# Row sums on one core: the last 8 rows of a partition in four loads of other sizes

## The chip, the cores and the metric

The kernel runs on 1 core of one Trainium2 chip. The metric is device time in microseconds (us) of one execution; the time before is the median of 3 runs. The profile is of one execution, and its times count from the first recorded instruction of that execution.

## The reference

```
def setup_inputs():
    batch, seq, dim = 32, 512, 1024
    return {"x": np.random.randn(batch, seq, dim).astype(np.float32)}

def reference(x):
    return np.sum(x, axis=-1).astype(np.float32)
```

The input has 32 x 512 = 16384 rows of 1024 float32 values (67.1 MB), and the output is one sum for each row (64 KB).

## The kernel before

The 16384 rows are spread over 128 partitions, 128 rows each. A row that is in SBUF is summed along its 1024 values by one of two engines, and the sums are collected in the tile `sums` (128 partitions x 128 values). Partition p holds 16 rows of a first region (the rows 0 to 15 of `sums`) and 112 rows of a second one (16 to 127); within a region the rows of a partition follow each other in DRAM, so that every load reads one contiguous run for each partition.

**Loads.** All loads of x are issued on SP's queue, in program order, into three rotating tiles `t` of 16 rows (and 4 values) each (pool `in`, `bufs=3`, line 145). The first load (lines 202 to 204) brings the first `FIRST` = 7 rows of the last 16; one of the hooks that run on the built program (lines 10 to 28) puts this load at the program's entry. Then come seven loads of 16 rows, g = 0 to 6 (lines 206 to 211, issued on line 192). The load of g = 1 is held until the first sum on DVE is done (line 213). What is left of the last 16 rows, 9 rows, comes as four loads: 6 rows (line 216), 2 rows (line 217), and the last row in two column pieces of 536 and 488 values (lines 227 and 228). A load into a tile waits until the tile's former user, three tiles back, has been read.

**Sums.** DVE sums the first 7 rows and the six groups g = 0 to 5 with one `tensor_reduce` each (`vec`, line 153). From g = 6 on, DVE takes single rows with `halves` (line 167): one instruction adds the two halves of a row and accumulates the total, so it runs over 512 elements for a row of 1024; a second small instruction reads the accumulator out. ACT takes whole rows with an activation that accumulates (`act`, line 180). Of g = 6, DVE has 9 rows and ACT 7; of the 6 rows, DVE 4 and ACT 2; of the 2 rows, one each. The last row is on DVE alone: the sum of its first 536 values is written as a `carry` into the cell in front of the 488 values, and the second `halves` sums that cell, the 488 values and one zeroed cell behind them (490 values, 245 elements; lines 223 to 233). The second instruction thus reads what the first one's accumulator read has written, and it waits for it by a semaphore of DVE's own.

**Stores.** ACT's queue issues two stores (lines 229 and 231): the 96 sums of the second region that are done by then, held until the load of 2 rows has landed, and the 16 sums of the first region. SP's queue issues the last store (line 234), the last 16 sums, when DVE and ACT have finished the rows. At the program's end GpSimd waits for that store to land (lines 55 to 98). The order on each engine is the order of the program text (`tc.manual_schedule()`).

Of the kernel before, what the change touches and what calls it, by code (L numbers as in the profile page):

```python
# [100 lines left out]
@with_exitstack  # L101
def kernel(
    ctx: ExitStack,
    tc: tile.TileContext,
    x: bass.AP,
    out: bass.AP,
):
    nc = tc.nc
    nc.at_finalize(issue_first_load_at_entry)
    nc.at_finalize(order_waits)  # L110
    nc.at_finalize(wait_for_the_store_at_the_clear)
    fp32 = mybir.dt.float32
    P = 128
    batch, seq, dim = x.shape
    rows = batch * seq
    J = rows // P
    BIG = 16


    x_r = x.flatten_outer_dims()  # L120
    out_r = out.rearrange("b s -> (b s)")
    ONE = BIG
    TWO = J - ONE

    def region(first, n):
        lo, hi = first * P, (first + n) * P
        return (
            x_r[lo:hi, :].rearrange("(p j) d -> p j d", j=n),
            out_r[lo:hi].rearrange("(p j) -> p j", j=n),
        )  # L130

    x_a, out_a = region(0, ONE)
    x_b, out_b = region(ONE, TWO)

    def rows_from(j, n):
        if j < ONE:
            return x_a[:, j : j + n, :]
        return x_b[:, j - ONE : j - ONE + n, :]

    last = J // BIG - 1  # L140
    FIRST = 7
    pieces = (536, 488)

    with (
        tc.tile_pool(name="in", bufs=3) as inpool,
        tc.tile_pool(name="unread", bufs=4, space=bass.MemoryType.PSUM) as upool,
        tc.tile_pool(name="stage", bufs=1) as stpool,
        tc.manual_schedule(),
    ):
        sums = stpool.tile([P, J], fp32)  # L150

        def vec(dst, src):
            return nc.vector.tensor_reduce(  # L153
                out=dst, in_=src, axis=mybir.AxisListType.X, op=mybir.AluOpType.add
            )

        def hold(inst, until, reason):
            tc.add_manual_dep(
                inst.ins,
                until.ins.name,  # L160
                mybir.DependencyInfo(mybir.DependencyClass.Sync, mybir.DependencyReason.DATA),
                reason=reason,
            )

        def halves(dst, src):
            n = src.shape[-1] // 2
            return nc.vector.tensor_tensor_reduce(  # L167
                out=src[:, :n],
                in0=src[:, :n],
                in1=src[:, n:],  # L170
                scale=1.0,
                scalar=0.0,
                op0=mybir.AluOpType.add,
                op1=mybir.AluOpType.add,
                accum_out=dst,
            )

        def act(dst, src, n):
            unread = upool.tile([P, dim], fp32)
            nc.scalar.activation(  # L180
                out=unread[:, :n],
                in_=src,
                func=mybir.ActivationFunctionType.Copy,
                accum_out=dst,
            )

        sums_of = []

        def rows(t, a, n, j, n_act, pairs=False):
            nv = n - n_act  # L190
            block = t[:, a * dim : (a + n) * dim].rearrange("p (n d) -> p n d", d=dim)
            load = nc.sync.dma_start(out=block, in_=rows_from(j, n))  # L192
            if pairs:
                for q in range(nv):
                    sums_of.append(halves(sums[:, j + q : j + q + 1], block[:, q, :]))
            else:
                sums_of.append(vec(sums[:, j : j + nv], block[:, :nv, :]))
            for q in range(nv, n):
                act(sums[:, j + q : j + q + 1], block[:, q, :], dim)
            return load  # L200

        j = last * BIG
        t = inpool.tile([P, BIG * dim + 4], fp32)
        rows(t, 0, FIRST, j, 0)
        first = sums_of[-1]
        for g in range(last):
            t = inpool.tile([P, BIG * dim + 4], fp32)
            if g < last - 1:
                load = rows(t, 0, BIG, g * BIG, 0)
            else:  # L210
                rows(t, 0, BIG, g * BIG, 7, pairs=True)
            if g == 1:
                hold(load, first, "no descriptors of later loads while the first ones start")

        t = inpool.tile([P, BIG * dim + 4], fp32)
        rows(t, FIRST, 6, j + FIRST, 2, pairs=True)
        two = rows(t, FIRST + 6, 2, j + FIRST + 6, 1, pairs=True)
        a = BIG - 1

        j += a
        c, width = pieces
        whole = t[:, a * dim + c : BIG * dim + 2]
        nc.vector.memset(whole[:, width + 1 :], 0.0)  # L225
        part = t[:, a * dim : a * dim + c]
        nc.sync.dma_start(out=part, in_=rows_from(j, 1)[:, 0, :c])  # L227
        nc.sync.dma_start(out=whole[:, 1 : width + 1], in_=rows_from(j, 1)[:, 0, c:])
        early = nc.scalar.dma_start(out=out_b[:, : TWO - BIG], in_=sums[:, ONE : J - BIG])
        hold(early, two, "its packets come behind those of the loads")  # L230
        nc.scalar.dma_start(out=out_a, in_=sums[:, :ONE])
        halves(whole[:, :1], part)
        halves(sums[:, j : j + 1], whole)
        nc.sync.dma_start(out=out_b[:, TWO - BIG :], in_=sums[:, J - BIG :])


# [28 lines left out]
```

## Time and profile before

| what | value |
|---|---|
| time, median of 3 runs (lowest to highest) | 161.54 us (161.33 to 161.68) |
| span of the profiled execution | 159.5 us |
| what lies between that span and the median | 2.0 us |
| DVE busy | 120.6 us (76%) in 40 instructions |
| ACT busy | 11.9 us (7%) in 21 instructions |
| SP's load queue, share of the 16 DMA engines | 97.8%, 67.12 MB |

The span runs from the first to the last instruction of the profiled execution; no time of that execution other than its span is listed, so the 2.0 us outside it is taken from the median. The chain of work that ended last is followed back from the last instruction, at each step to what released it. A `halves` shows as two records, `CUSTOM_DVE_ANT_0` (the sum) and `DVE_READ_ACCUMULATOR2_ANT` (the read-out, some 0.08 us). A load "lands" when the last of its completion counts has arrived.

### The profile page before, as it was taken

What the parts mean: (1) busy time and instruction counts of PE and PEld (TensorE: products, weight loads), DVE (VectorE), ACT (ScalarE), POOL (GpSimd) and SP (SyncE); (2) the same over time, 40 slices, a digit from 0 to 9 for tenths busy, and PEclk for the clock granted to TensorE, in tenths of its full rate; (3) what the DMA queues carried; (4) which work ended last, traced back from release to release, by engine and by line L of the source; (5) the groups of instructions that cost most, each with busy time, mean ns of one, the idle gap of its engine ahead of it and who ended that gap; (6) DMA issues with size and microseconds to landing.
All of it is one profiled execution on the core that took longest, in us unless ns stands there. A gap on an engine that the chain in (4) does not pass through costs nothing.

```text
span 159.5 us, 133 instructions
## 1 busy us (share of the span) xinstructions
DVE 120.6 (76%) x40; ACT 11.9 (7%) x21; POOL 0.2 (0%) x4
## 2 busy tenths in 40 slices
DVE  0029600499985999779995899949999499994955
ACT  3000000000000000000000000000000000003993
POOL 0000000000000000000000000000000000000000
DMA  8899989799699699699699699897996996996993
GB/s 316 388 479 526 411 378 526 329 460 526 279 509 526 263 526 526 263 526 526 263 526 493 296 526 427 362 526 345 444 526 279 509 526 263 526 526 283 407 384 125
DMA packets 2160, 67.18 MB, mean 421 GB/s; under 512 B 624, under 2 KB 752, under 8 KB 880
## 3 DMA queue, kind: packets, MB, share of 16 engines
q1 hardware_dynamic: 1872, 67.12, 97.8%
q10 hardware_dynamic: 288, 0.06, 0.2%
HBM read 67.11 MB, written 0.07 MB: 421 GB/s over the span
## 4 chain that ended last, share of the span: by engine, by line
DMA 71%; DVE 27%; SPq 1%; issue 0%; DVEq 0%
DMA t<-in_x_dram 71%; DVE sums L153 26%; SPq L192 0%; SPq L227 0%; DVE t L167 0%; DVEq L260 0%
## 5 line engine op out<-in xcount | busy, mean ns | idle before, releaser
L153 DVE TENSOR_REDUCE sums<-t 128x16 f32<-128x16384 f32 (+1 forms) x7 | 110.9, 15849 | 33.2 <-DMA t<-in_x_dram 33.2
L180 ACT ACTIVATE unread<-t 128x1024 f32<-128x1024 f32 x10 | 10.1, 1011 | 144.6 <-DMA t<-in_x_dram 144.6
L167 DVE CUSTOM_DVE_ANT_0 t<-t 128x512 f32<-128x512 f32 (+2 forms) x16 | 9.6, 657 | 4.0 <-DMA t<-in_x_dram 3.8
L180 ACT ACTIVATION_READ_ACCUMULATOR unread<-t 128x1 f32 x10 | 1.9, 186 | 0.0
L180 ACT ACT_TABLE_LOAD x1 | 1.3, 1283 | 0.8 <-PEq L249 0.8
L167 DVE DVE_READ_ACCUMULATOR2_ANT sums<- 128x1 f32 x15 | 1.3, 84 | 0.0
L249 POOL MEMSET const-bfloat16-1.0<- 128x1 bf16 x1 | 0.1, 101 | 0.0
L249 POOL MEMSET const-uint8-127<- 128x1 uint8 x1 | 0.1, 101 | 0.0
L249 POOL MEMSET const-float32-0.0<- 128x1 f32 x1 | 0.1, 98 | 0.2 <-issue 0.2
L249 POOL MEMSET const-float32-1.0<- 128x1 f32 x1 | 0.1, 98 | 0.0
L167 DVE DVE_READ_ACCUMULATOR2_ANT t<- 128x1 f32 x1 | 0.1, 81 | 0.0
L225 DVE MEMSET t<- 128x1 f32 x1 | 0.1, 59 | 0.0
## 6 DMA issues: line engine op xcount, KB each, us to landing
t<-in_x_dram SPq DMA_DIRECT2D x1, 3584.0 KB, 10.8
t<-in_x_dram SPq DMA_DIRECT2D x1, 3072.0 KB, 28.7
t<-in_x_dram SPq DMA_DIRECT2D x1, 1024.0 KB, 30.9
t<-in_x_dram SPq DMA_DIRECT2D x1, 268.0 KB, 31.0
t<-in_x_dram SPq DMA_DIRECT2D x1, 244.0 KB, 31.2
t<-in_x_dram SPq DMA_DIRECT2D x7, 40.8
out_dram<-sums ACTq DMA_DIRECT2D x1, 48.0 KB, 1.6
out_dram<-sums ACTq DMA_DIRECT2D x1, 8.0 KB, 1.5
```

The costliest lines, as they stand in the source:

```text
L153: return nc.vector.tensor_reduce(out=dst, in_=src, axis=mybir.AxisListType.X, op=mybir.AluOpType.add)
L167: return nc.vector.tensor_tensor_reduce(out=src[:, :n], in0=src[:, :n], in1=src[:, n:], scale=1.0, scalar=0.0, op0=mybir.AluOpType.add, op ...
L180: nc.scalar.activation(out=unread[:, :n], in_=src, func=mybir.ActivationFunctionType.Copy, accum_out=dst,)
L225: nc.vector.memset(whole[:, width + 1 :], 0.0)
L249: nc = _bacc.Bacc("TRN2", target_bir_lowering=False, num_devices=1)
```

## The change

`FIRST` becomes 8, so that 8 rows of 1024 values = 8192 values are left for each partition. They are taken as one run of values, with no regard to rows, in four loads of 5504, 1920, 512 and 256 values. Row boundaries are at 1024, 2048 and so on, so that row 5 (5120 to 6143) is cut at 5504, and row 7 (7168 to 8191) at 7424 and at 7936. Rows 3, 4 and 6 of the eight go to ACT, and the other five to DVE. Between two loads the tile has a gap of 2 cells: one zeroed, and one for the carry of the part of the row in front of it. A `halves` over the later part of a cut row starts at these two cells. Of g = 6, ACT has 6 rows in place of 7, and DVE 10 in place of 9.

The built program has on DVE, behind the 10 rows of g = 6: three memsets of one cell, `halves` of 512, 512, 512 and 192 elements (rows 0, 1, 2 and the first part of 5), then 321 and 128 (the rest of 5, the first part of 7), 257 (the second part of 7) and 129 (its last part). The 321, the 257 and the 129 each wait both for a load and for the carry of the `halves` that wrote it. On SP the four loads stand where four loads stood; on ACT 9 activations stand in place of 10, with the two stores behind them. In the text the two stores are now issued between the third and the fourth load, and the first is held until the load of 1920 values has landed.

```
-    FIRST = 7
-    pieces = (536, 488)
+    FIRST = 8
+    GAP = 2
+    LATE = ((0, 5504, (3, 4)), (5504, 1920, (6,)), (7424, 512, ()), (7936, 256, ()))
+    assert sum(n for _, n, _ in LATE) == (BIG - FIRST) * dim
...
+        def loads_end(q):
+            return LATE[q][0] + LATE[q][1]
...
-                rows(t, 0, BIG, g * BIG, 7, pairs=True)
+                rows(t, 0, BIG, g * BIG, 6, pairs=True)
...
+        j += FIRST
+        flat = rows_from(j, BIG - FIRST).rearrange("p n d -> p (n d)")
         t = inpool.tile([P, BIG * dim + 4], fp32)
-        rows(t, FIRST, 6, j + FIRST, 2, pairs=True)
-        two = rows(t, FIRST + 6, 2, j + FIRST + 6, 1, pairs=True)
-        a = BIG - 1
-        j += a
-        c, width = pieces
-        whole = t[:, a * dim + c : BIG * dim + 2]
-        nc.vector.memset(whole[:, width + 1 :], 0.0)
-        part = t[:, a * dim : a * dim + c]
-        nc.sync.dma_start(out=part, in_=rows_from(j, 1)[:, 0, :c])
-        nc.sync.dma_start(out=whole[:, 1 : width + 1], in_=rows_from(j, 1)[:, 0, c:])
-        early = nc.scalar.dma_start(out=out_b[:, : TWO - BIG], in_=sums[:, ONE : J - BIG])
-        hold(early, two, "its packets come behind those of the loads")
-        nc.scalar.dma_start(out=out_a, in_=sums[:, :ONE])
-        halves(whole[:, :1], part)
-        halves(sums[:, j : j + 1], whole)
+        for q, (at, _, _) in enumerate(LATE[1:], 1):
+            nc.vector.memset(t[:, at + (q - 1) * GAP : at + (q - 1) * GAP + 1], 0.0)
+        loads = []
+        for q, (at, n, on_act) in enumerate(LATE):
+            shift = q * GAP
+            loads.append(nc.sync.dma_start(out=t[:, at + shift : at + shift + n], in_=flat[:, at : at + n]))
+            if q == 2:
+                early = nc.scalar.dma_start(out=out_b[:, : TWO - BIG], in_=sums[:, ONE : J - BIG])
+                hold(early, loads[1], "its packets come behind those of the loads")
+                nc.scalar.dma_start(out=out_a, in_=sums[:, :ONE])
+            while at < loads_end(q):
+                row = at // dim
+                stop = min((row + 1) * dim, loads_end(q))
+                total = sums[:, j + row : j + row + 1]
+                if row in on_act:
+                    act(total, t[:, at + shift : stop + shift], dim)
+                else:
+                    start = at + shift - (GAP if at % dim else 0)
+                    whole = stop % dim == 0
+                    carry = t[:, stop + shift + 1 : stop + shift + 2]
+                    halves(total if whole else carry, t[:, start : stop + shift])
+                at = stop
         nc.sync.dma_start(out=out_b[:, TWO - BIG :], in_=sums[:, J - BIG :])
```

## Prediction

> **What bounds the kernel now.** I read the chain of work that ended last first. From the span's start it goes load, sum, load, sum, and from 126.16 us on it is this (columns: start, length, what):
>
> ```profile
> 125.68 0.43 SPq L227
> 126.11 0.04 issue
> 126.16 31.16 DMA t<-in_x_dram
> 157.32 0.02 issue
> 157.34 0.42 DVE t L167
> 157.76 0.01 DVEq L260
> ```
>
> The last load lands at 157.32, one sum of 0.42 us follows, and the last store goes out. The sums that the chain names earlier (DVE, 26% of the span) are not the limit. The table by stages shows it; the first row is one group of 16 rows, from landing to landing, and the others are the stages between the landings of g = 6, of the 6 rows, of the 2 rows, of the 536 and of the 488 values (columns: window, length, busy time with instruction count of DVE, ACT and POOL, clock, DMA share, GB/s):
>
> ```profile
> 107.55:126.91 19.36, 17.22 (x1) 0.00 (x0) 0.00 (x0) 1.00 1.00 433
> ...
> 146.26:153.56 7.30, 5.60 (x18) 7.28 (x14) 0.00 (x0) 1.00 0.99 425
> 153.56:156.07 2.51, 2.48 (x8) 2.21 (x5) 0.00 (x0) 1.00 0.98 398
> 156.07:156.73 0.66, 0.66 (x4) 0.64 (x1) 0.00 (x0) 1.00 0.86 330
> 156.73:157.32 0.59, 0.47 (x5) 0.51 (x2) 0.00 (x0) 1.00 0.33 89
> ```
>
> The DMA engines are full until the last packets (share 1.00 in the middle), and DVE needs 17.22 of 19.36 us. So the bytes set when the last data lands, and the change moves the same bytes. What it can alter is the packets' overhead and the **tail**: what is left to do when the last data has landed. The tail is in the timeline (start, length, engine, line, operation):
>
> ```profile
> 156.09 0.69 DVE L167 CUSTOM_DVE_ANT_0 t<-t 128x512 f32<-128x512 f32 x1
> 156.71 0.08 DVE L167 DVE_READ_ACCUMULATOR2_ANT sums<- 128x1 f32 x1
> 156.74 0.06 DVE L225 MEMSET t<- 128x1 f32 x1
> 156.75 0.44 DVE L167 CUSTOM_DVE_ANT_0 t<-t 128x268 f32<-128x268 f32 x1
> 157.05 0.19 ACT L180 ACTIVATION_READ_ACCUMULATOR unread<-t 128x1 f32 x1
> 157.11 0.08 DVE L167 DVE_READ_ACCUMULATOR2_ANT t<- 128x1 f32 x1
> 157.34 0.42 DVE L167 CUSTOM_DVE_ANT_0 t<-t 128x245 f32<-128x245 f32 x1
> 157.68 0.08 DVE L167 DVE_READ_ACCUMULATOR2_ANT sums<- 128x1 f32 x1
> 157.79 0.35 SPq L234 DMA_DIRECT2D out_dram<-sums  x1
> ```
>
> Two things are to be seen. An independent sum starts when the read-out of the sum before it starts (from 156.09 to 156.71 is 0.61, though the record is 0.69 long). But the 245-element sum depends on the carry of the 268: the read-out ended at 157.195, and the sum started at 157.344, 23 ns after the landing at 157.321. Between them stands DVE's wait for its own semaphore, which the records put at 157.234 with 21 ns. So a **hand-over** g from the end of one `halves` to the start of the next that reads its carry is at least 0.06 us (157.255 less 157.195) and at most 0.15. In this kernel the data comes last anyway, and the hand-over costs nothing.
>
> **Part 1, bytes and packets.** Each load has one packet for each partition, 8 on each of 16 engines, one behind the other. Landing to landing, divided by 8, gives the price of one: 24576 B (6 rows) 7.30/8 = 0.912; 8192 B 2.51/8 = 0.313; 2144 B 0.66/8 = 0.082; 1952 B 0.59/8 = 0.074. Between these, 22016 B (5504 values) is 0.819, 7680 B 0.295 and 2048 B 0.078. 1024 B lies between the 384 B packets of the early store (0.022) and 1952 B: 0.043 on the line, 0.022 to 0.074 as bounds. Times 8: 6.55, 2.36, 0.62 and 0.34, in sum 9.87. Before, the four took 157.32 - 146.26 = 11.06. The first load has packets of 32768 B in place of 28672 B: at 27.3 B per ns (from the 8192 and 24576 B prices) +0.150 each, +1.20 in all. Sum: 9.87 + 1.20 - 11.06 = 0.01, that is zero: **the last data lands at 157.32 as before** (157.2 to 157.6 by the bounds on 1024 B). The landings from which the rest is worked out: g = 6 at 146.26 + 1.20 = 147.46; 5504 at 154.01; 1920 at 156.37; 512 at 156.99; 256 at 157.32.
>
> **Part 2, the front.** The first load lands at 10.79 + 1.20 = 12.0, its sum of 8 rows takes 7.62 + 1.07 = 8.7 and ends at 20.7 in place of 18.43. The held load of g = 1 is issued 2.3 us later; g = 0 is in flight until 31.4, so this is hidden by 10 us. All groups shift by 1.20, DVE's idle of 2.1 us before each stays, and SP issues the four late loads at about 126.0 to 127.8 (0.43 each), 20 us ahead of their first packet. Cost: nothing.
>
> **Part 3, the last group and the 5504 values.** DVE: 10 rows from 147.48, 0.613 apart, end at 153.7 and the three memsets at 153.9; ACT: 6 rows of 1.04 end at 153.7. Both are ready before 154.01. Cost nothing; the cover is 0.1 to 0.3 us, and if it were gone, what is late would first use up the slack below. From 154.04 DVE runs three rows (1.84) and the 192 elements (record 0.36) to 156.24; with the hand-over it is ready for the 321 at 156.30 to 156.39, against a landing at 156.37. ACT's rows 3 and 4 end at 156.15.
>
> **Part 4, the tail.** A sum from its start to that of its read-out is 0.613 (512), 0.364 (268) and 0.339 (245 elements): 1.03 ns for an element and 0.088 fixed, near the 0.06 to 0.085 of the rows with one element (memset, read-out). So 321: 0.417; 257: 0.352; 128: 0.219; 129: 0.220; the read-out adds 0.081. For the two smallest no row exists; the bounds are 0.08 (one element) and 0.339 (245), and I take the line, as it meets the rows at both ends. DVE from the landing of the 1920 values:
> - 321 starts at 156.39; the independent 128 follows at 156.81 and ends, with its read-out, at 157.11
> - 257 needs that carry: it starts at 157.11 + g and takes 0.433. Its data landed at 156.99, so the carry decides
> - 129 needs the carry of the 257: it starts at 157.54 + 2g and takes 0.301. Its data landed at 157.32; again the carry decides
> - end 157.84 + 2g, against 157.76 before: **+0.08 + 2g**
>
> The bounds on g give +0.20 to +0.38. I take g = 0.09: a waiting instruction started 23 ns after its semaphore, and ACT's store record started 38 ns behind its wait record, so 0.06 + 0.03. That makes **+0.26**. What is queued behind the waiting sums on DVE is only the rest of this chain, and SP's last store waits for it. The bounds on 128 and 129 add -0.28 to +0.24, though below -0.08 the landing and ACT set the end.
>
> Beside it: ACT's row 6 starts at 156.39, takes 1.03 and its read-out to 157.54, hidden under DVE's 158.02. The two stores on ACT's queue go out 0.30 later (156.48, 156.89) and land at about 158.08 and 158.42; their packets start 0.9 after issue, at 157.36, behind the last load's packets, and the last store lands at about 159.48, so they are hidden. From SP's issue to the end it is as before, 159.53 - 157.79 = 1.74.
>
> Sum: span 159.53 + 0.26 = 159.79. The median shown lies 2.01 above the span, and I take that as fixed: **161.80 us**, +0.16%. The three runs shown spread over 0.35 us; 0.2% of the time (0.32 us) is about what a measurement of this kernel can tell from no change.
>
> **A rule to weigh.** The trace has dependent sums once, with g between 0.06 and 0.15, and independent ones that overlap by 0.08. The Trainium skill, VectorE: DVE Perf Modes, section "The DRAIN you can't avoid", says that each DVE instruction waits for the pipe to empty in any case, so that a semaphore between two of them costs nothing extra. By it, g would be what independent sums show. That is the first rival; the wait record that ends 0.06 after the read-out speaks against it.
>
> **Rivals.**
> - *The hand-over is free.* With g = 0 the end is +0.08 (161.62); with the overlap of independent sums, the 257 starts at 157.03, the 129 at 157.38, and the end is 157.68, -0.08 (161.46). Then the shorter last sum is a gain of a tenth of a us. For it: DVE is a queue in order. Against: the wait record. Chance 0.15.
> - *The hand-over or the small sums are dear: slower.* Place: between the 128 and the 257 and between the 257 and the 129. Price: at g = 0.15 the end is +0.38 (161.92). With the two small sums at the price of 245 elements and g = 0.09 it is +0.50 (162.04). It decides from g = 0.12, where +0.08 + 2g passes 0.32. For it: the trace allows 0.15, and a wait that finds its semaphore set is not seen there. Chance 0.27.
> - *The stream lands late.* If 1024 B cost as much as 1952 B, the last data lands 0.25 later, at 157.57, and the 129 would start at 157.72 anyway: hidden. Only if the 1920 values are late (packets to cells shifted by 8 B, or a slow first load) does it move the tail, one for one: 0.2 late is 162.0. Against: the 488 values, put one cell off, cost no more per byte than the 536. Chance 0.05.
>
> **How the numbers follow.** The forecast, +0.20 to +0.32, has 0.53; the rivals have 0.15, 0.27 and 0.05. Faster by over 0.2% needs 161.2: no mechanism above reaches it, only the spread of the runs on top of the free hand-over, 0.07. Slower by over 0.2%: the two dear cases, with the forecast's upper edge and the spread, 0.38. Within: 0.55. The range takes in both ends, with the spread at the low one: 161.35 to 162.10.
>
> **What would show it.** Right: landings near 147.46, 154.01, 156.37 and 157.32; a 257-element sum that starts about 0.09 after the 128's read-out has ended, not 0.02 after its landing; the same before the 129; DVE's last record ending near 158.02 and the chain naming DVE, not DMA, for the last 1.6 us. Wrong: a 129 that starts right behind the last landing, a span below 159.5, or a last landing over 0.4 us later.

## The result and the profile after

The changed kernel takes **162.18 us** (median of 4 runs, 162.15 to 162.21), against 161.52 for the kernel before (4 runs, 161.33 to 161.68). The ratio is 1.0042, with a 95% interval of 1.0031 to 1.0054: slower by 0.66 us, 0.4%. The forecast was 161.80 in a range of 161.35 to 162.10, most likely within 0.2%. The direction of the working was right, and the size was not: the time lies above the range.

The chain of work that ended last, in the profile after (start, length, what), from the issue of the load of 1920 values on:

```profile
126.47 29.98 DMA t<-in_x_dram
156.46 0.02 issue
156.48 0.49 DVE t L171
156.97 0.01 DVE sums L171
156.98 0.22 DVE t L171 x2
157.20 0.03 issue
157.23 0.02 DVEq L171
157.25 0.08 issue
157.34 0.45 DVE t L171 x2
157.78 0.03 issue
157.81 0.02 DVEq L171
157.83 0.08 issue
157.91 0.29 DVE t L171
158.21 0.01 DVEq L276
```

Before, the chain came to its last sum from the last landing. Now it leaves the DMA at the landing of the 1920 values, 156.46, and stays on DVE: four sums, and twice the same stretch of 0.03 issue, 0.02 wait on DVE's sequencer (DVEq) and 0.08 issue. That is the hand-over. Neither of the two landings that come later is in the chain. The stages between the landings of g = 6 and of the four loads (window, length, DVE, ACT, POOL, clock, DMA share, GB/s), behind one full group:

```profile
108.82:128.18 19.36, 17.22 (x1) 0.00 (x0) 0.00 (x0) 1.00 1.00 433
147.56:154.10 6.54, 6.24 (x23) 6.35 (x12) 0.00 (x0) 1.00 1.00 426
154.10:156.46 2.36, 2.20 (x8) 2.19 (x4) 0.00 (x0) 1.00 0.97 397
156.46:157.15 0.69, 0.67 (x4) 0.67 (x1) 0.00 (x0) 1.00 0.50 171
157.15:157.45 0.30, 0.16 (x3) 0.30 (x2) 0.00 (x0) 1.00 0.00 1
```

The lengths of 6.54, 2.36, 0.69 and 0.30 are near those worked out (6.55, 2.36, 0.62 and 0.34), and the last data lands at 157.45. The tail in the timeline after (DVE and SP):

```profile
156.90 0.29 DVE L171 CUSTOM_DVE_ANT_0 t<-t 128x128 f32<-128x128 f32 x1
...
157.11 0.08 DVE L171 DVE_READ_ACCUMULATOR2_ANT t<- 128x1 f32 x1
157.34 0.43 DVE L171 CUSTOM_DVE_ANT_0 t<-t 128x257 f32<-128x257 f32 x1
...
157.69 0.08 DVE L171 DVE_READ_ACCUMULATOR2_ANT t<- 128x1 f32 x1
157.91 0.29 DVE L171 CUSTOM_DVE_ANT_0 t<-t 128x129 f32<-128x129 f32 x1
158.13 0.08 DVE L171 DVE_READ_ACCUMULATOR2_ANT sums<- 128x1 f32 x1
158.24 0.35 SPq L250 DMA_DIRECT2D out_dram<-sums  x1
```

By the records of the packed trace, which go to the ns, the 128's read-out ends at 157.191 and the 257 starts at 157.335; the 257's ends at 157.770 and the 129 starts at 157.914. Both hand-overs are **0.144 us**.

SP's last issue moved from 157.795 to 158.243, 0.45 later, and the span from 159.5 to 160.0. The time grew by 0.66. The rest lies **outside the span**: each run comes with its time and its span (to 0.1 us), and in the four runs after, time less span is 2.15 to 2.21 us. For the kernel before it is 1.73 to 1.83 in all the runs of the experiments. So the two profiles explain 0.4 to 0.5 us, and the remainder needs another cause.

### The profile page after: what moved, and what is told of

Read it like the earlier page. It is cut to its first block, busy times and chain, and to the rows that moved or that the text cites. A ratio compares the mean times of both kernels' runs of the same rounds, so it can differ in the third digit from the quotient of the medians.

```text
span 160.0 us, 138 instructions
## 1 busy us (share of the span) xinstructions
DVE 121.9 (76%) x46; ACT 11.0 (7%) x19; POOL 0.2 (0%) x4
## 4 chain that ended last, share of the span: by engine, by line
DMA 71%; DVE 28%; issue 0%; SPq 0%; DVEq 0%
DMA t<-in_x_dram 71%; DVE sums L157 27%; DVE t L171 1%; SPq L232 0%; DVEq L171 0%; DVEq L276 0%; DVE sums L171 0%
## 5 line engine op out<-in xcount | busy, mean ns | idle before, releaser
L184 ACT ACTIVATE unread<-t 128x1024 f32<-128x1024 f32 x9 | 9.1, 1014 | 145.9 <-DMA t<-in_x_dram 145.9
L171 DVE CUSTOM_DVE_ANT_0 t<-t 128x512 f32<-128x512 f32 (+5 forms) x18 | 9.8, 598 | 2.9 <-DMA t<-in_x_dram 2.6
```

Source lines behind the costliest of these rows:

```text
L171: return nc.vector.tensor_tensor_reduce(out=src[:, :n], in0=src[:, :n], in1=src[:, n:], scale=1.0, scalar=0.0, op0=mybir.AluOpType.add, op ...
L184: nc.scalar.activation(out=unread[:, :n], in_=src, func=mybir.ActivationFunctionType.Copy, accum_out=dst,)
```

## The experiments

The first theory was that the hand-overs cost the 0.4 us of the tail, and that the rest was the place of one profiled execution within the spread of the kernel before. The rival was the front: that the larger first load delays the stream, or the program's start.

**The kernel before, unchanged.**

> The kernel before, unchanged, to see how its profile and time differ from one execution to the next. Both theories: 161.5 us. The hand-over theory explains 0.37 of the 0.66 us that the change cost (two waits of 0.144 us and 0.08 of work between the landing of the 1920 values and the last store); the rest, 0.13 us of later landings and 0.2 us outside the span, would be the place of one profiled execution of the kernel before within its spread of 0.35 us. Then this profile's span is 159.3 to 159.6 and time less span is about 2.2, as it was for the changed kernel. The front theory (the larger first load delays the stream and the start) has time less span at 2.0 here.

Measured: 161.41 us (11 runs) against 161.44 (32 runs), ratio 0.9992 to 1.0010; time less span 1.75 to 1.83. That part of my expectation failed: the kernel before has 1.8 us outside the span in every run, so the 2.2 us of the changed kernel are no spread of one execution. The chain's end in this profile:

```profile
157.38 0.06 issue
157.44 0.42 DVE t L167
157.85 0.01 DVEq L260
```

The last sum started 0.06 after the last landing, not 0.02. By the records, the 268's read-out ended at 157.293, and 0.145 later is 157.438, where the sum started. In this execution the hand-over decided in the kernel before as well, by 0.04.

**One part at a time: the front alone, the tail alone.** The first puts the old tail behind a first load of 8 rows:

```
-    FIRST = 7
+    FIRST = 8
-                rows(t, 0, BIG, g * BIG, 7, pairs=True)
+                rows(t, 0, BIG, g * BIG, 6, pairs=True)
-        rows(t, FIRST, 6, j + FIRST, 2, pairs=True)
-        two = rows(t, FIRST + 6, 2, j + FIRST + 6, 1, pairs=True)
+        rows(t, FIRST, 5, j + FIRST, 2, pairs=True)
+        two = rows(t, FIRST + 5, 2, j + FIRST + 5, 1, pairs=True)
```

> The first load of 8 rows and 6 rows of the last group on ACT, as changed, but the tail of before: 5 rows, 2 rows, 536 and 488 values. Hand-over theory: the 245-element sum again starts at the last landing, so 161.5 us, within 0.1 of before. Front theory (the larger first load is what costs): 161.8 to 162.2 us.

Measured: 161.43 us, ratio 0.9996 to 1.0013. The front costs nothing that shows. The second starts from the changed kernel:

```
-    FIRST = 8
+    FIRST = 7
-    LATE = ((0, 5504, (3, 4)), (5504, 1920, (6,)), ...
+    LATE = ((0, 1024, ()), (1024, 5504, (4, 5)), (6528, 1920, (7,)), (8448, 512, ()), (8960, 256, ()))
-                rows(t, 0, BIG, g * BIG, 6, pairs=True)
+                rows(t, 0, BIG, g * BIG, 7, pairs=True)
-            if q == 2:
+            if q == 3:
-                hold(early, loads[1], ...
+                hold(early, loads[2], ...
```

> The first load of 7 rows as before and 7 rows of the last group on ACT, then one row in a load of its own, and the four late loads of 5504, 1920, 512 and 256 values as changed. Hand-over theory: the tail costs 0.37 us, 161.9 us, with the 257 and the 129 elements starting 0.144 us after the read-outs before them. Front theory: 161.5 us.

Measured: 161.83 us, 0.39 over the kernel before, ratio 1.0015 to 1.0035; time less span 1.8. The tail alone costs what the hand-over theory says (0.37 us and 161.9 were expected), and the front theory falls.

**One hand-over more in the kernel before.**

```
-    pieces = (536, 488)
+    pieces = (280, 256, 488)
...
+        halves(second[:, :1], part)
-        halves(whole[:, :1], part)
+        halves(whole[:, :1], second)
         halves(sums[:, j : j + 1], whole)
```

> The kernel before with the last row in three pieces of 280, 256 and 488 values, each sum reading the carry of the one before, in place of 536 and 488. Nothing else is changed, and the last piece is the same. Hand-over theory: 140 elements end at 157.04, 129 start at 157.19, 245 at 157.63, end 158.05, that is 0.29 us over before, 161.8 us. If hand-overs were free, the 245 would start at the last landing as before: 161.5 us.

Measured: 161.71 us, 0.27 over before, ratio 1.0008 to 1.0025. The chain shows the two stretches of 0.13, with nothing of the changed kernel's loads in it:

```profile
157.25 0.03 issue
157.28 0.02 DVEq L167
157.30 0.08 issue
157.38 0.31 DVE t L167 x2
157.69 0.03 issue
157.72 0.02 DVEq L167
157.74 0.08 issue
157.83 0.41 DVE t L167
```

**The changed kernel again, beside its own parts.** The next four ran on one chip.

> The changed kernel, unchanged, beside runs of the kernel before on the same chip. The first result had 2.2 us outside the span in each of four runs, where the runs of the last four kernels had 1.8. If that is a matter of the chip or session and not of the program, 1.8 us lie outside the span here too, and the change costs what its tail costs: 0.37 us by the hand-over theory, 161.8 us against 161.44. If it belongs to the program, 162.1 us or more.

Measured: 162.16 us against 161.33, ratio 1.0035 to 1.0059; time less span 2.16 to 2.24. The 2.2 us belong to the program. Beside 23 runs of the kernel before, the change costs 0.83 us, about one half in the span and one half outside it. The 0.66 of the result rests on four runs of the kernel before that spread over 0.35 us. The next kernel swaps the order of two waits, in the hook that sorts them (`order_waits`):

```
+            if isinstance(inst, mybir.InstCustomDveAnt) and any(
+                (w.ant_name or "").startswith(("DMAHW2", "DMAHW3")) for w in inst.sync_info.on_wait
+            ):
+                insts[k] = with_first(inst, "DVE")
-            if isinstance(inst, (mybir.InstActivation, mybir.InstCustomDveAnt)):
+            elif isinstance(inst, (mybir.InstActivation, mybir.InstCustomDveAnt)):
```

> The changed kernel with the two waits of the 257 and of the 129 elements in the other order: the load's wait goes ahead as an instruction of its own, and the wait for the carry rides on the sum itself. Both waits are kept. If the 0.144 us of a hand-over is mostly the way from a wait instruction that ends late to the sum behind it, a sum that carries the wait itself starts some 0.035 us after the read-out (0.012 to the semaphore, 0.023 to the start), each hand-over is 0.11 shorter, and the time is 161.6 us. If it is the dependence itself, the pipe that has to empty, nothing changes: 161.8 us.

Measured: 161.96 us, 0.20 under the changed kernel beside it (6 and 5 runs, whose ranges overlap). The forecast time of 161.6 was missed, since 2.2 us lie outside the span here as well and not 1.8; what the two hand-overs lost is in its timeline:

```profile
157.14 0.08 DVE L175 DVE_READ_ACCUMULATOR2_ANT t<- 128x1 f32 x1
157.31 0.43 DVE L175 CUSTOM_DVE_ANT_0 t<-t 128x257 f32<-128x257 f32 x1
...
157.66 0.08 DVE L175 DVE_READ_ACCUMULATOR2_ANT t<- 128x1 f32 x1
157.78 0.29 DVE L175 CUSTOM_DVE_ANT_0 t<-t 128x129 f32<-128x129 f32 x1
```

The second hand-over is 157.781 less 157.746, 0.035 us, for the same dependence. The first is 0.09, because the load's own wait now stands ahead: it ended at 157.227, 0.05 after the landing at 157.177, and the sum started 0.084 after it. So most of the 0.144 is the wait as an instruction of its own, with the 0.084 from its end to the next start; the dependence alone leaves 0.035. The two hand-overs lost 0.16 us together, where 0.22 was expected.

The next kernel has one hand-over less:

```
-                    start = at + shift - (GAP if at % dim else 0)
+                    start = at + shift - (GAP if at % dim and q != 2 else 0)
-                    carry = t[:, stop + shift + 1 : stop + shift + 2]
+                    cell = LATE[3][0] + 2 * GAP if stop == LATE[2][0] else stop + shift + 1
+                    carry = t[:, cell : cell + 1]
```

> The changed kernel in which the 512 values are summed without the carry of row 7's first part (256 elements, no wait on DVE); that carry goes to the cell that was the zero in front of the last 256 values, so the last sum reads two carries. One hand-over of two is left behind the 1920 values' landing. Hand-over theory: the 256 elements start at their landing, 157.17, in place of 157.34, and the end is 0.17 us earlier: 161.6 us. If hand-overs were not the price, 161.8 us.

Measured: 161.59 us. That is the time expected, but in part by luck: of the 0.57 us under the changed kernel, 0.4 come from outside the span (1.8 here), which the working did not have, and the span's median is 0.2 shorter (159.8 for 160.0). In its profile, of an execution whose stream came later, the 256 elements start 0.024 after their landing and the last sum 0.144 after the read-out ahead of it, as the theory has it. The last one reads no carry at all (`start = at + shift`):

> The changed kernel with the carries written but not read: the sums of rows 5 and 7 of the last eight leave out their earlier parts. The loads, the pieces and the number of sums are the same, and no sum waits for another. Hand-over theory: the last sum starts at or just behind the last landing and is shorter than before's, so 161.36 us, 0.08 under before and 0.45 under the changed kernel. If the loads' sizes or the number of sums are the price, 161.7 to 161.8 us.

Measured: 161.32 us against 161.33, ratio 0.9991 to 1.0008; time less span 1.8. The same loads and pieces with no hand-over run as fast as the kernel before, though their sums leave out parts of two rows. Its timeline:

```profile
157.19 0.43 DVE L171 CUSTOM_DVE_ANT_0 t<-t 128x256 f32<-128x256 f32 x1
157.47 0.19 ACT L184 ACTIVATION_READ_ACCUMULATOR unread<-t 128x1 f32 x1
157.54 0.08 DVE L171 DVE_READ_ACCUMULATOR2_ANT t<- 128x1 f32 x1
157.54 0.29 DVE L171 CUSTOM_DVE_ANT_0 t<-t 128x128 f32<-128x128 f32 x1
```

The last sum starts together with the read-out ahead of it, 0.08 after the last landing (157.46): here DVE's own pace sets the end.

**The 0.4 us outside the span.** So far two programs had 2.2 us outside the span, the changed kernel and the one with swapped waits. Both have 58 instructions on DVE, counted in the built program with waits, branches and closing instructions (the traces record two fewer in every program); the others have 51, 55 and 59. The next four add memsets of cells that nobody reads, in DVE's idle time behind the first sum, so that nothing else moves:

```
         first = sums_of[-1]
+        pad = stpool.tile([P, 8], fp32)
+        for q in range(1):
+            nc.vector.memset(pad[:, 2 * q : 2 * q + 1], 0.0)
```

> The changed kernel with one more instruction on DVE: a memset of one cell that nobody reads, behind the first sum, where DVE idles for 11 us. So far the time less the span is 2.2 us for the two programs with 58 instructions in DVE's program (the changed kernel with its waits in either order) and 1.8 us for those with 51, 55 and 59. Theory of the place: the number of DVE's instructions decides what lies outside the span, with 3 left over after division by 4 at 1.8 and 2 left over at 2.2. This one has 59: 1.8 us outside, 161.75 us in all, 0.4 under the changed kernel, at the same span of 160.0. Rival: the 0.4 us belongs to the two hand-overs behind each other at the end of DVE's program: 2.2 us, 162.15 us.

> The kernel before with three such memsets, 54 instructions on DVE, 2 left over after division by 4. Theory of the place: 2.2 us outside the span, 161.8 us. Rival (the hand-overs, or the changed tail): 1.8 us, 161.4 us.

> The kernel before with one such memset, 52 instructions on DVE, none left over after division by 4. Theory of the place: another value than 1.8 us is possible, between 1.4 and 2.6, and if it is below 1.8 this beats the kernel before. Rival: 1.8 us, 161.4 us.

> The kernel before with two such memsets, 53 instructions on DVE, 1 left over after division by 4. Theory of the place: between 1.4 and 2.6 us outside the span. Rival: 1.8 us, 161.4 us.

Measured: the changed kernel with one memset more takes **161.72 us** (ratio to the kernel before 1.0009 to 1.0042), 0.4 less than without it on another chip, with 1.8 us outside (59 instructions). The rival, two hand-overs behind each other at the program's end, falls, since they are still there. But 52, 53 and 54 instructions in the kernel before all have 1.8 (161.34, 161.44 and 161.33 us, no ratio's interval clear of 1), so the remainder after division by 4 was wrong too. Three kernels more (the memset of the second on GpSimd, `nc.gpsimd.memset`):

> The kernel before with seven memsets of cells that nobody reads, behind the first sum: 58 instructions on DVE, as the changed kernel has. If the exact number of DVE's instructions puts 0.4 us outside the span, 2.2 us lie there and the time is 161.8 us at an unchanged span of 159.6. If it takes the changed tail as well, 1.8 us, 161.4 us.

> The changed kernel with such a memset on GpSimd in place of DVE: DVE keeps 58 instructions, the whole program has two more (GpSimd's memset and a wait of SP's at the end). If DVE's number decides, 2.2 us outside the span, 162.15 us. If the whole program's number or place decides, 1.8 us, 161.75 us.

> The changed kernel with two such memsets on DVE: 60 instructions there. If 58 alone is an unlucky number, 1.8 us outside the span, 161.75 us. If even numbers of the changed kernel are, 2.2 us, 162.15 us.

Measured: the kernel before with 58 instructions takes 161.77 us, ratio 1.0006 to 1.0030, at a span of 159.6 and with 2.16 to 2.22 outside. Its chain ends as that of before, so that the span tells nothing of the 0.4 us:

```profile
157.38 0.02 issue
157.41 0.42 DVE t L167
157.82 0.01 DVEq L263
```

With the extra memset on GpSimd the changed kernel keeps 2.2 (162.10 us), and with 60 instructions on DVE it has 1.88 to 1.96 (161.86 us). All three programs have 140 recorded instructions in all, so the whole program's number does not decide; DVE's does, in either kernel. The last three:

> The kernel before with six memsets on DVE, 57 instructions there. If what lies outside the span hangs on single numbers (58 at 2.2, 59 at 1.8, 60 at 1.9), 57 can be anything from 1.8 to 2.2 us; 1.8, as at 55 and below, would make 58 the first such number: 161.4 us. 161.8 us if 57 has it as well.

Measured: 161.77 us, ratio 1.0016 to 1.0036, 2.13 to 2.22 outside: 57 instructions have the 0.4 us too.

> The changed kernel with the two waits of the last two sums in the other order, and one memset more on DVE (59 instructions). In the profile of swapped_waits the 257 started 0.09 and the 129 0.035 us after the read-outs before them, in place of 0.144 each. Hand-over theory: 0.16 us less than after_plus1, 161.55 us. If the end does not hang on the hand-overs: 161.7 us.

Measured: 161.56 us, 1.8 outside: 0.16 under after_plus1, as expected, though that one ran on another chip (0.18 and 0.33 over the kernel before beside each). The ratio to the kernel before is 1.0007 to 1.0025.

> The changed kernel with one hand-over (as in one_handover, 55 instructions on DVE), and the last sum's two waits in the other order, so that this hand-over is 0.035 us in place of 0.144. Hand-over theory: 0.11 us less than one_handover, 161.48 us, within 0.1 of the kernel before. If the order of the waits did nothing: 161.6 us.

The edit is that of swapped_waits for the last sum alone. Measured: 161.43 us against 161.38, ratio 0.9992 to 1.0009. Its chain's end:

```profile
157.38 0.02 issue
157.40 0.09 DVE t L175
157.49 0.02 issue
157.51 0.29 DVE t L175
157.81 0.01 DVEq L281
```

One hand-over is left, with 0.02 of issue in place of 0.13. The changed loads then cost nothing, but no version here is faster than the kernel before.

**Where the 0.4 us lies.** The chains end with the last instruction, but the packed traces also hold the updates of semaphores behind it. In every profile the last of them are nine updates of semaphore 2, which no instruction of the kernel names; they begin 1.55 us after the last instruction's end. Between the fifth and the sixth lie 0.10 us with up to 55 and with 59 instructions on DVE, and 0.52 in all five profiles with 58. With 60, the third and the fourth lie 0.19 apart instead of 0.04. The updates of this semaphore in the last 0.4 us ahead of the span agree to 0.003 in all of them. So with 58 and 60 the extra time is spent at the program's end, behind the last instruction. The profile with 57 shows neither gap, though its execution had 2.2 us outside the span: there the place stays open.

All runs at a glance (medians; outside: time less span):

| kernel | DVE instructions | time | before beside it | span | outside |
|---|---|---|---|---|---|
| before, again | 51 | 161.41 | 161.44 | 159.6 | 1.8 |
| first load of 8, old tail | 51 | 161.43 | 161.44 | 159.6 | 1.8 |
| before + 1, + 2, + 3 memsets | 52, 53, 54 | 161.34, 161.44, 161.33 | 161.39 | 159.5 to 159.7 | 1.8 |
| before + 6 memsets | 57 | 161.77 | 161.38 | 159.6 | 2.2 |
| before + 7 memsets | 58 | 161.77 | 161.37 | 159.6 | 2.2 |
| before, three pieces | 55 | 161.71 | 161.44 | 159.9 | 1.8 |
| changed, the result | 58 | 162.18 | 161.52 | 160.0 | 2.2 |
| changed, again | 58 | 162.16 | 161.33 | 160.0 | 2.2 |
| changed + 1 on GpSimd | 58 | 162.10 | 161.37 | 159.9 | 2.2 |
| changed + 1, + 2 memsets | 59, 60 | 161.72, 161.86 | 161.39, 161.37 | 159.9 | 1.8, 1.9 |
| first load of 7, new tail | 59 | 161.83 | 161.44 | 160.0 | 1.8 |
| swapped waits | 58 | 161.96 | 161.33 | 159.8 | 2.2 |
| swapped waits + 1 memset | 59 | 161.56 | 161.38 | 159.8 | 1.8 |
| one hand-over | 55 | 161.59 | 161.33 | 159.8 | 1.8 |
| one hand-over, swapped | 55 | 161.43 | 161.38 | 159.6 | 1.8 |
| no carry | 55 | 161.32 | 161.33 | 159.5 | 1.8 |

## Why the prediction was right and wrong, point by point

- **The bytes and packets: right.** "The last data lands at 157.32 as before": it landed at 157.45, and every stage was within 0.07 of its length. The 0.1 us came with the front, and the kernel before varies by half as much (157.32 and 157.38 in its two profiles).
- **The front and the last group cost nothing: right** (first8_old_tail, 161.43 against 161.44).
- **The tail, +0.08 + 2g: right in form.** DVE's sums took 0.49, 0.29, 0.43 and 0.29, as worked out, the end hung on the two carries, and the chain named DVE. With g = 0.144 the formula gives +0.37; first7_new_tail, which has the tail alone, measured +0.39, and after_plus1 +0.33.
- **g = 0.09: this step failed in size.** It was "0.06 + 0.03", with the 0.03 from two other rows (0.023 from a semaphore to a sum, 0.038 from a wait to a store on ACT). What lies between DVE's wait record and the next DVE start is 0.084, so g is 0.144, at the upper bound that the trace of before gave (0.15). That bound had hardly any slack: 157.255 + 0.084 = 157.339 is within 0.005 of where the last sum started before (157.344), so there the hand-over and the landing came almost together. I took the hand-over to be hidden behind the landing, and the row showed nearly its whole length.
- **"The median shown lies 2.01 above the span, and I take that as fixed": this step failed.** The 2.01 were one profiled execution against the median of others. The kernel before has 1.8, which the fastest of the three runs shown also gives (161.33 less 159.5). And it is not fixed: it is 2.2 in every kernel run with 57 or 58 instructions on DVE, and the change took DVE from 51 to 58. That is 0.4 us, about as much as the tail costs.
- **How the two add up.** The forecast was 159.79 + 2.01, and the profiled execution after has 160.0 + 2.2. Of the 0.38 us between them, half is in the span: 0.11 from g, and 0.09 because the 1920 values landed at 156.46 and not at 156.37. The other half is outside. Neither half alone would have left the range, which ends at 162.10. The 2.01 was 0.2 too high for the kernel before, and by luck this hid half of the 0.4: with 1.8 the same working gives 161.59. So it is luck in part, too, that 161.72, the time at 59 instructions, is close to the forecast of 161.80: the span was 0.1 longer and the rest 0.2 shorter than worked out.
- **The rival of the free hand-over fell**, and the rule beside it did not hold here. The Trainium skill, VectorE: DVE Perf Modes, section "The DRAIN you can't avoid", has a semaphore between two DVE instructions cost nothing extra, as measured on a chain of eight copies. Here a sum without one starts 0.08 before the read-out ahead of it has ended, one whose wait rides on it 0.035 after, and one behind a wait instruction 0.144 after. The measurement decides: the wait costs.
- **The rival of the dear hand-over was the right mechanism and came close in price** (g = 0.15 and +0.38, with 0.27 as its chance); it too took what lies outside the span as fixed.
- **The rival of the late stream** had its condition in small: the 1920 values were 0.09 late in the profile after and moved the tail by as much. In the other profiles with the changed loads they land between 156.27 and 157.04, so this is spread between executions; the last landing never set the end of the changed kernel's profiles.

What stays open is why 57 and 58 instructions on DVE add 0.4 us, and 60 add 0.1. The extra time lies behind the last instruction with 58 and 60, and no record names what is done there. A stall in the fetching of instructions at the program's end is a guess: the Trainium skill, Runtime: NRT & Kernel Launch, section "Instruction fetch mechanics", says that instructions are fetched in blocks and that a branch to a place outside the fetched pages stalls, but no run here shows a fetch there, and 59 instructions are free of it.

## What to carry to other kernels

Price a chain of dependent sums by its hand-overs, and look which of two waits rides on the instruction: the one that ends last should, since a wait that stands ahead on its own costs 0.1 us more when it is the late one. A price that seems hidden behind something else may be as large as the row allows, until its end is shown to have come earlier than what hid it. For differences of some tenths of a us, compare time less span between the two kernels before the traces: here about half of the loss, 0.4 us, lay outside the span, and one idle instruction more took it away.

## What the runs showed of the hardware that was not expected

- A wait that precedes a DVE sum as its own instruction: in the tails read here it starts 0.027 to 0.029 after the semaphore and takes 0.021, and where nothing later holds the sum, the sum starts 0.084 or 0.085 after its end. A sum that carries its wait starts 0.023 or 0.024 after the semaphore. The Trainium skill, Perfetto Trace Analysis, section "DVE / Act Engine Instruction (TENSOR_ADD, Activation, etc)", has a DVE instruction decoded and pushed to a queue where it waits; this fits both numbers, as behind a wait of the sequencer the decoding would come after it, though the profile does not record it.
- The number of instructions in DVE's program moves the time outside the span: 1.8 us at 51 to 55 and at 59, 2.2 at 57 and 58, 1.9 at 60. At 58 it is the same in two kernels that differ in their loads and sums, and at 59 in three.
